# A hybrid sequence block on one core: the opening stage re-ordered, with its input rows turned on TensorE

## The chip, the core and the metric

The kernel runs on one core of a Trainium2 chip. The metric is the device time of one execution in microseconds (us), given as the median of three runs. The core's engines are TensorE (PE, matrix products), VectorE (DVE), ScalarE (ACT), GpSimd (POOL) and SyncE (SP, which here only issues transfers). Each engine works through its own list of instructions in order and waits where an operand or a buffer isn't ready.

## What is computed

One layer on x of 2048 rows by 1024: a norm of the rows, one combined projection, three groups (an mLSTM with gates, a pooling group, attention to 256 memory rows), an output projection and a final norm. What the change touches are the two norms and the memory's keys and values:

```
def rmsnorm(x, g):
    xf = x.astype(jnp.float32)
    y = xf * lax.rsqrt(jnp.mean(xf * xf, axis=-1, keepdims=True) + EPS)
    return (y * g.astype(jnp.float32)).astype(x.dtype)
...
    mn = rmsnorm(mem, mem_norm_g)
    kv = mn @ w_kv
    km, vm = jnp.split(kv, 2, axis=-1)
```

## The kernel before

**Products.** Each fp32 operand is split in two reduced-precision parts, hi (a copy, made by ACT) and lo (the difference to it, made by DVE), and each product is three matmuls: hi by hi, hi by lo, lo by hi (`mm3`, lines 150 to 156). A projection of a 1024x1024 block of x is cut into quarters A11, A12, A21, A22 (block of 512 rows by half of the 1024 columns), and done in seven products in place of eight: A11, A12, A22 and four sums of quarters, S1 to S4. With the blocks a, b (first) and c, d (second): S1 = c + d, which the code calls `e`; S2 = e - a; S3 = a - c; S4 = b - S2. The weights have forms of their own in the same way (T1 to T3, N4). Such a projection is a `Quad`; `TOK_ORDER` gives the order of its products, and a list `stream` sets when the forms of its weights are made (`pump`, `prep`).

**Halves.** The 2048 rows are done in two halves, s = 0 and s = 1. A half needs its seven forms of x, each [128 partitions, hi/lo, 512] in four pieces k; x stands there with columns on the partitions and rows along the free axis. The `y` tiles hold the unsplit quarters.

**Opening stage (lines 560 to 626).** It makes the forms of the first half and does one projection with them (`run_tok`), and the keys and values of the memory beside it. Memory comes transposed (`memT`, line 484), is split (490, 491) and squared (493), and the squares are summed by products with one column of ones (495). Rows of x come twice: once as rows for the sum of squares (`block_rows`, 500 to 507, ACT), once transposed (`load_y_raw`, line 178). `rsqrt_mean` (158 to 161) makes the factor of each row, with the power on POOL; `bcast` (163 to 169) puts the factors along the free axis by a product of diagonal tiles `dg` with ones, and `scale_y` (184 to 191) multiplies x by it on DVE. `x_split` (193 to 200) and `x_steps` (202 to 222) make the forms; POOL adds `e` and subtracts for S4, DVE does the other sums. Memory keys (`mem_k`, 525 to 530, four products of 24 matmuls) and values (`mem_v`, 541 to 548) lie between the products of x, hung on a count of products (`first(n)`, 596 to 622). The gates' product (`gates`, 450 to 476; one 16-column weight by A11, A12, S3 and A22) comes at the start of the next stage.

**What sets the order.** The program is written in this order, but a scheduler places the instructions of each engine, except those pinned by `keep_in_program_order`. PSUM tiles come from tags (`mm`, `pt`, `aux`), each with two buffers where the opening uses them. Working tiles are reused by tag, so a tile's next user waits for the last reader.

Of the kernel before, what the change touches and what calls it, by code (L numbers as in the profile page):

```python
# [18 lines left out]
P = 128  # L19
SEQ = 2048  # L20
# [32 lines left out]
def hybrid_block(tc, xT, xn, memT, wch, wuT, wtok, wgt, wkm, wvm, wo, pw, cols, bg, gf, out):  # L53
# [33 lines left out]
    with ExitStack() as outer:  # L87
# [18 lines left out]
        rm = const([P, MT], "rm")  # L106
        gat = const([P, NT, 8], "gat")
# [94 lines left out]
        def x_steps(y):  # L202
# [6 lines left out]
            return {  # L209
                "A11": lambda: x_split("A11", a),  # L210
# [13 lines left out]
        class Quad:  # L224
            def __init__(self, kind, s, i):
                self.kind, self.s, self.i = kind, s, i
                self.tok = kind == "tok"
                self.order = TOK_ORDER if self.tok else CH_ORDER
# [51 lines left out]
            def prep(self, f):  # L280
# [109 lines left out]
        def run_tok(q, step=None, pinned=False):  # L390
# [9 lines left out]
            for n, (xfm, wfm, acc, opens) in enumerate(q.order):  # L400
# [5 lines left out]
                for bk in range(2):  # L406
# [9 lines left out]
                    if n == 0:  # L416
                        s1[bk] = ev("s1")
                        A.activation(s1[bk], pf, AF.Copy)
                    elif n == 1:
# [3 lines left out]
                    elif n == 2:  # L423
                        u2[bk] = ev("u2")
                        V.tensor_tensor(u2[bk], pf, s1[bk], ALU.add)
                    elif n == 3:
                        V.tensor_tensor(s1[bk], pf, u2[bk], ALU.add)
                    elif n == 4:
# [5 lines left out]
                    elif n == 5:  # L434
# [15 lines left out]
        def gates(s):  # L450
            g1, g2 = bank([P, BW], "aux"), bank([P, BW], "aux")
            gs = [ev(f"gs{i}", tag="u2") for i in range(2)]

            def prod(pp, f, wt, k0, first, last):
                for k in range(4):
                    w = wt[:, (k0 + k) * 16:(k0 + k) * 16 + P]
                    T.matmul(pp, w, xf[f][k][:, 0], start=first and k == 0, stop=False, skip_group_check=True)
                    T.matmul(pp, w, xf[f][k][:, 1], start=False, stop=last and k == 3, skip_group_check=True)
            prod(g1, "A11", wgp, 0, True, True)
            ga = ev("ga")  # L460
            V.tensor_copy(ga[0:16], g1[0:16])
            prod(g2, "S3", wgn, 0, True, False)
            prod(g1, "A12", wgp, 4, False, True)
            V.tensor_copy(gs[0][0:16], g1[0:16])
            prod(g2, "A22", wgp, 4, False, True)
            V.tensor_tensor(gs[1][0:16], g2[0:16], ga[0:16], ALU.add)

            def finish_gates():
                for i in range(2):
                    b = 2 * s + i  # L470
                    pg = bank([P, 4, 8], "aux")
                    for t in range(4):
                        T.matmul(pg[:, t], gs[i][0:16, t * P:(t + 1) * P], e16[0:16], start=True, stop=True)
                    V.tensor_tensor(gat[:, 4 * b:4 * b + 4], pg, bgb.unsqueeze(1).to_broadcast([P, 4, 8]), ALU.add)
            return finish_gates
# [4 lines left out]
        def mem_load():  # L480
            pr = bank([P, MT], "pt")
            for i in range(4):
                raw = xslot(8 + i, [P, 2, NMEM], "mraw")
                dma(raw, memT[2 * i:2 * i + 2].rearrange("k p m -> p k m"))
# [111 lines left out]
        def first(n):  # L596
# [13 lines left out]
            elif 3 <= n < 7:  # L610
# [5 lines left out]
                if n < 5:  # L616
                    Wv.append(mem_w(wvm[n - 1], [P, 2, GW]))
# [647 lines left out]
```

## Time and profile before

| | us |
|---|---|
| median of three runs | 1221.77 (1220.72 to 1221.81) |
| profiled execution | 1220.8 |
| its span, first to last instruction | 1218.9 |
| PE busy | 1173.5 (96%) |
| DVE busy | 743.9 (61%) |
| ACT busy | 480.5 (39%) |
| POOL busy | 211.5 (17%) |
| mean granted clock of PE | 0.983 of full |

PE is the busy engine of the whole. The mean hides the stages: the profile's strip of 40 slices shows PE at six and seven tenths in the first three slices of 30 us and at nine in nearly all others, and the granted clock under full in those three alone. The views read below are windows of the span, the waits of PE by what ended them, and the timelines of the engines in the opening stage.

### The profile page before, as it was taken

How to read it: one execution, taken by the hardware profiler on the slowest of the kernel's cores; microseconds unless marked ns; L12 is line 12 of the kernel's file. 1: busy time of each engine (PE TensorE's matmuls, PEld its weight loads, DVE VectorE, ACT ScalarE, POOL GpSimd, SP SyncE). 2: the span in 40 equal slices, each digit the busy share in tenths (PEclk: the TensorE clock that was granted, in tenths of full speed). 3: DMA queues.
4: the chain of work that ended last, by engine and by line, in shares of the span. 5: the costliest groups of instructions: out<-in, count | busy, mean ns of one | idle time of the engine just before them, and what ended most of it. 6: DMA issues, size and time to landing. Idle time of an engine off the chain costs nothing. (4 is left out here: it accounts for less than half of the span.)

```text
span 1218.9 us, 17628 instructions
## 1 busy us (share of the span) xinstructions
PE 1173.5 (96%) x6579; PEld 1016.1 (83%) x6579; DVE 743.9 (61%) x1324; ACT 480.5 (39%) x947; POOL 211.5 (17%) x154
## 2 busy tenths in 40 slices
PE   6769999999999999999999999999999999999997
PEld 5759888887888998998788888888978888888886
DVE  5966587887777559633564554554546656556444
ACT  7534544444766444331311225555433223222211
POOL 1351121112001003100000000000054423233110
PEclk9879999999999999999999999999999999999999
DMA  9618788779555796546667776446695454554411
GB/s 350 233 44 299 265 293 281 259 276 324 211 195 182 256 390 226 181 140 228 198 219 241 240 244 226 154 155 223 214 325 188 137 184 154 172 165 151 144 52 69
DMA packets 124725, 258.75 MB, mean 212 GB/s; under 512 B 9824, under 2 KB 66400, under 8 KB 124384
## 3 DMA queue, kind: packets, MB, share of 16 engines
q1 hardware_dynamic: 83232, 226.17, 53.9%
q10 hardware_dynamic: 41408, 31.46, 8.1%
q8 instruction: 52, 0.85, 0.3%
q14 instruction: 33, 0.27, 0.1%
HBM read 158.96 MB, written 98.63 MB: 211 GB/s over the span
## 5 line engine op out<-in xcount | busy, mean ns | idle before, releaser
L307 ACT ACTIVATE wf<-wr 128x512 fp32r<-128x512 f32 x120 | 74.3, 627 | 106.7 <-PE mm L156 56.1
L308 DVE TENSOR_TENSOR wf<-wr,wf 128x512 fp32r<-128x512 f32 x120 | 84.8, 716 | 35.2 <-ACT wf L307 35.1
L152 PE MATMUL mm<-xS,wf 128*128 128x512 f32 x256 | 101.3, 396 | 1.9 <-DVE s L377 1.9
L156 PE MATMUL mm<-xS,wf 128*128 128x512 f32 x256 | 101.7, 397 | 0.0
L155 PE MATMUL mm<-xS,wf 128*128 128x512 f32 x256 | 101.0, 395 | 0.0
L1025 PE MATMUL mm<-woh,ybh 128*128 128x512 f32 x256 | 94.8, 405 | 0.0
L1025 PE MATMUL mm<-wol,ybh 128*128 128x512 f32 x256 | 92.8, 397 | 0.0
L1025 PE MATMUL mm<-woh,ybl 128*128 128x512 f32 x256 | 89.9, 394 | 0.0
L152 PE MATMUL mm<-xA,wf 128*128 128x512 f32 x224 | 88.6, 396 | 0.0
L156 PE MATMUL mm<-xA,wf 128*128 128x512 f32 x224 | 87.9, 393 | 0.0
L155 PE MATMUL mm<-xA,wf 128*128 128x512 f32 x224 | 87.7, 392 | 0.0
L1129 DVE SCALAR_TENSOR_TENSOR hh<-hh,ss,gz 128x128 f32<-128x128 f32 x64 | 52.4, 878 | 31.1 <-POOL ss L1127 31.1
L647 DVE SCALAR_TENSOR_TENSOR cacc<-text,col,cacc 128x1024 f32<-128x1024 f32 x48 | 65.5, 1374 | 6.7 <-ACT cacc L644 6.5
L996 POOL TENSOR_TENSOR ybl<-yr,ybh 128x1024 fp32r<-128x1024 f32 x16 | 39.2, 2450 | 173.2 <-ACT ybh L995 169.7
L291 POOL TENSOR_TENSOR wr<-wr 128x512 f32<-128x512 f32 (+1 forms) x16 | 27.2, 1697 | 198.8 <-DVE wf L308 180.4
L152 PE MATMUL pt<-wf,xS 128*128 128x256 f32 x192 | 55.7, 290 | 5.7 <-ACT xS L198 4.6
L156 PE MATMUL pt<-wf,xS 128*128 128x256 f32 x192 | 55.5, 289 | 5.2 <-DVE xS L199 5.2
L156 PE MATMUL mm<-wf,xA 128*128 128x256 f32 x192 | 56.3, 293 | 3.7 <-DVE xA L199 3.7
L152 PE MATMUL mm<-wf,xA 128*128 128x256 f32 x192 | 57.1, 297 | 2.0 <-DMA wf<-d_tok1B 2.0
L152 PEld LDWEIGHTS mm<-xS,wf 128*128 128x128 f32 x256 | 48.5, 189 | 12.0 <-DVE s L377 2.4
L156 PEld LDWEIGHTS mm<-xS,wf 128*128 128x128 f32 x256 | 48.6, 190 | 10.9
L155 PEld LDWEIGHTS mm<-xS,wf 128*128 128x128 f32 x256 | 48.5, 189 | 10.1
(314 smaller groups left out, 3251.3 us busy)
## 6 DMA issues: line engine op xcount, KB each, us to landing
wr<-in_wch_dram SPq DMA_DIRECT2D x20, 512.0 KB, 5.8
y<-in_xT_dram SPq DMA_DIRECT2D x32, 256.0 KB, 6.9
wr<-in_wtok_dram SPq DMA_DIRECT2D x16, 512.0 KB, 6.0
d_qk<-cacc ACTq DMA_DIRECT2D x32, 256.0 KB, 4.5
yr<-d_y SPq DMA_DIRECT2D x16, 512.0 KB, 4.7
qk<-d_qk SPq DMA_DIRECT2D x16, 512.0 KB, 4.1
gz<-d_t SPq DMA_DIRECT2D x16, 512.0 KB, 3.7
xr<-in_xn_dram SPq DMA_DIRECT2D x16, 512.0 KB, 3.6
```

What stands on the lines that cost most here:

```text
L152: ins = T.matmul(po, ah, bh, start=first, stop=False, skip_group_check=True)
L155: T.matmul(po, ah, bl, start=False, stop=False, skip_group_check=True)
L156: T.matmul(po, al, bh, start=False, stop=last, skip_group_check=True)
L291: G.tensor_tensor(B["B11"], B["B12"], B["B11"], ALU.subtract)
L307: A.activation(t[:, 0], part, AF.Copy)
L308: V.tensor_tensor(t[:, 1], part, r32(t[:, 0]), ALU.subtract)
L647: V.scalar_tensor_tensor(c, t[:, i:i + 2 * BW], w(i), c, ALU.mult, ALU.add)
L996: G.tensor_tensor(yl, yr, r32(yh), ALU.subtract)
L1025: T.matmul(outs[c][n], l, w[:, n * 512:(n + 1) * 512], start=i == 0 and p_ == 0, stop=i == KO - 1 and p_ == 2)
L1129: V.scalar_tensor_tensor(hh[:, h], hh[:, h], ss[:, h:h + 1], gz[:, 1, h], ALU.mult, ALU.mult)
```

## The change

- The first half's x is no longer loaded transposed. Its rows come once, 128 rows (512 KB) at a time. Their squares are summed alternately on ACT and on DVE, POOL makes the power, and DVE scales the rows where they are.
- PE turns the scaled rows, 128x128 at a time, into PSUM. From there ACT makes hi, DVE makes lo, and ACT makes a plain copy; the norm's weights are applied on the way. For the second block, DVE makes `e` straight from PSUM.
- The memory rows come, are scaled and are turned in the same way, after the second block of x.
- The first half's gate products of A11 and A12 follow the turning of the second block; those of S3 and A22 follow the opening's projection. In the second half both stand at the start of its stage.
- S1's product comes before S2's in the first projection.
- Memory keys and values come last; their weights are split in pieces of 512 instead of 1024.

Cut to its core:

```diff
+FIRST_ORDER = TOK_ORDER[:2] + (TOK_ORDER[3], TOK_ORDER[2]) + TOK_ORDER[4:]
...
-                self.order = TOK_ORDER if self.tok else CH_ORDER
+                self.order = CH_ORDER if not self.tok else TOK_ORDER if s or i else FIRST_ORDER
...
-                if f == "T2":
+                if f in ("T1", "T2") and "T1" not in B:
                     G.tensor_tensor(B["B11"], B["B12"], B["B11"], ALU.subtract)
                     B["T1"] = B["B11"]
+                if f == "T2":
...
+                    elif xfm in ("S2", "S1"):
+                        if xfm == "S2":
+                            u2[bk] = ev("u2")
+                            V.tensor_tensor(u2[bk], pf, s1[bk], ALU.add)
+                        if n == 3:
+                            V.tensor_tensor(s1[bk], banks["V"][bk].rearrange("p a b -> p (a b)"), u2[bk], ALU.add)
...
+        def gates_a(s):
+            g1 = bank([P, BW], "aux")
+            gate_prod(g1, "A11", wgp, 0, True, True)
+            ga[0] = ev("ga")
+            V.tensor_copy(ga[0][0:16], g1[0:16])
+            gate_prod(g1, "A12", wgp, 4, False, True)
+            gs = ev("gs", tag="u2") if s else xslot(19, [P, BW], "gs")
+            V.tensor_copy(gs[0:16], g1[0:16])
+            return gate_out(2 * s, gs)
+
+        def gates_b(s):
+            g2 = bank([P, BW], "aux")
+            gate_prod(g2, "S3", wgn, 0, True, False)
+            gate_prod(g2, "A22", wgp, 4, False, True)
+            gs = ev("gs", tag="u2")
+            V.tensor_tensor(gs[0:16], g2[0:16], ga[0][0:16], ALU.add)
+            return gate_out(2 * s + 1, gs)
...
+            def square(i):
+                junk = xslot(18 + (i % 2 if len(srcs) > 2 else 0), [P, D], "junk")
+                if i % 2:
+                    V.scalar_tensor_tensor(junk, rows[i], 1.0, rows[i], ALU.mult, ALU.mult, accum_out=sums[:, i:i + 1])
+                else:
+                    A.activation(junk, rows[i], AF.Square, accum_out=sums[:, i:i + 1])
+
+            def scale():
+                for j in range(0, len(srcs), 2):
+                    square(j)
+                    square(j + 1)
+                    rsqrt_mean(dst[:, j:j + 2], sums[:, j:j + 2], 2, D)
+                    for i in (j, j + 1):
+                        V.tensor_scalar(rows[i], rows[i], dst[:, i:i + 1], None, ALU.mult)
+            return rows, scale
...
+        def turn_rows(pt, rows, k):
+            for i, t in enumerate(rows):
+                ins = T.transpose(pt[:, i * P:(i + 1) * P], t[:, k * P:(k + 1) * P], ident)
+                if i == 0:
+                    tc.keep_in_program_order(ins)
...
+        def mem_load(rows):
+                pt = bank([P, 2, NMEM], "aux")
...
+                    turn_rows(pt[:, q], rows, k)
+                    A.activation(t[:, 0, q], pt[:, q], AF.Copy, scale=g)
+                    V.scalar_tensor_tensor(t[:, 1, q], pt[:, q], g, r32(t[:, 0, q]), ALU.mult, ALU.subtract)
...
+        def turned(rows, h):
+            for k in range(4):
+                pt = bank([P, BW], "pt" if k % 2 else "aux")
+                turn_rows(pt, rows, 4 * h + k)
+                yield k, pt, col[:, C_NG + 4 * h + k:C_NG + 4 * h + k + 1]
+
+        def block_form(y, rows, h):
+            f = ("A11", "A12")[h]
+            xf[f] = []
+            for k, pt, g in turned(rows, h):
+                t = xp.tile([P, 2, BW], F32R, name=f"x{f}_{k}", tag=f"x{4 * FORMS.index(f) + k}")
+                A.activation(t[:, 0], pt, AF.Copy, scale=g)
+                V.scalar_tensor_tensor(t[:, 1], pt, g, r32(t[:, 0]), ALU.mult, ALU.subtract)
+                A.activation(y[0][h][k], pt, AF.Copy, scale=g)
+                xf[f].append(t)
+
+        def block_y(y, rows, h, e=None):
+            for k, pt, g in turned(rows, h):
+                if e is not None:
+                    V.scalar_tensor_tensor(e[k], pt, g, y[1][0][k], ALU.mult, ALU.add)
+                A.activation(y[1][h][k], pt, AF.Copy, scale=g)
...
+        def mem_hl():
+            n = Wn[0]
+            Wn[0] += 1
+            hi = misc([P, 4 * P], "mwh", F32R, tag=f"ye{n % 2}")
+            lo = misc([P, 4 * P], "mwl", F32R, tag=f"ye{2 + n % 2}")
+            A.activation(hi, W[n], AF.Copy)
+            V.tensor_tensor(lo, W[n], r32(hi), ALU.subtract)
...
+        rows, scale = norm_rows([xn[t * P:(t + 1) * P] for t in range(4)], (4, 5, 6, 7), ssq[:, 0:4], rt[:, 0:4])
+        dma(col, cols)
         quads[0].load((0,))
+        rows1, scale1 = norm_rows([xn[t * P:(t + 1) * P] for t in range(4, 8)], (12, 13, 14, 15), ssq[:, 4:8], rt[:, 4:8])
+        dma(bgb, bg.partition_broadcast(P))
+        wgr = misc([P, KD, 8], "wgr")
+        dma(wgr, wgt)
+        load_upto(quads[0])
+        mrows, mscale = norm_rows([memn[i * P:(i + 1) * P] for i in range(MT)], (16, 17), ssm, rm)
+        for i in range(4):
+            mem_raw(wkm[i].rearrange("p a b -> p (a b)"), 20 + i)
...
+        scale()
+        pump(1)
+        block_form(y, rows, 0)
+        scale1()
+        block_form(y, rows, 1)
+        pump(2)
...
+            if n == 3:
+                block_y(y, rows1, 0)
+            elif n == 4:
+                block_y(y, rows1, 1, e)
+                xs["S1"]()
+                later(2, gates_a(0))
+                xs["S2"]()
+            elif n == 5:
+                mscale()
+                mem_load(mrows)
+            elif n == 6:
+                mem_k(0)
+            elif n == 7:
+                xs["S3"]()
+                mem_k(1)
+            elif n == 8:
+                mem_k(2)
+            elif n == 9:
+                mem_k(3)
+                for i in range(4):
+                    mem_raw(wvm[i].rearrange("p a b -> p (a b)"), 20 + i)
+            elif n == 10:
+                for q in range(4):
+                    mem_v(q)
+                xs["S4"]()
+            elif n == 11:
+                xs["A22"]()
...
         run_tok(next(it), pinned=True)
+        later(1, gates_b(0))
...
-            later(1, gates(s))
             if s:
+                later(1, gates_a(s))
+                later(1, gates_b(s))
```

The next listings show what stands in a row on an engine. In them `xA_0` is piece 0 of a quarter, `xS_0` of a sum, `wf` a split weight, `mhl` the split memory, `mwh` and `mwl` the split weights of memory.

PE at the start of the opening, before (the squares of memory, its first keys, the broadcast of the rows' factors, the first product of x):

```order
L495 MATMUL pt<-ones,msq 128x1 x16
L152 MATMUL mm<-mhl_143,mwh 128x256
L155 MATMUL mm<-mhl_143,mwh 128x256
L156 MATMUL mm<-mhl_143,mwl 128x256
...
L168 MATMUL aux<-dg,ones 128x512
...
L152 MATMUL mm<-wf,xA_0_281 128x256
L155 MATMUL mm<-wf,xA_0_281 128x256
L156 MATMUL mm<-wf,xA_0_281 128x256
```

PE at the start, after:

```order
L519 MATMUL aux<-ident,rows 128x128 x4
L519 MATMUL pt<-ident,rows 128x128 x4
L519 MATMUL aux<-ident,rows 128x128 x4
L519 MATMUL pt<-ident,rows 128x128 x4
L519 MATMUL aux<-ident,rows 128x128 x4
L519 MATMUL pt<-ident,rows 128x128 x4
L519 MATMUL aux<-ident,rows 128x128 x4
L519 MATMUL pt<-ident,rows 128x128 x4
L154 MATMUL mm<-wf,xA_0_212 128x256
L157 MATMUL mm<-wf,xA_0_212 128x256
L158 MATMUL mm<-wf,xA_0_212 128x256
```

Thirty-two transposes stand in the place of the memory's squares, keys and broadcast, and the product of A11 follows them directly.

DVE in the middle of the opening, where the sums of quarters are made, before (`ye` is `e`, `y_120` to `y_123` the pieces of a, `y_128` to `y_131` those of c):

```order
L191 SCALAR_TENSOR_TENSOR y_135<-y_135,col,aux 128x512
L308 TENSOR_TENSOR wf<-wr,wf 128x512 x2
L208 TENSOR_TENSOR y_128<-y_120,y_128 128x512
L199 TENSOR_TENSOR xS_0_775<-ye_136,xS_0_775 128x512
L208 TENSOR_TENSOR y_129<-y_121,y_129 128x512
L534 TENSOR_TENSOR kmt<-mm,rmb 128x256
L519 TENSOR_TENSOR mwl<-mwraw,mwh 128x1024
L208 TENSOR_TENSOR y_130<-y_122,y_130 128x512
L208 TENSOR_TENSOR y_120<-ye_136,y_120 128x512
L199 TENSOR_TENSOR xS_2_781<-ye_138,xS_2_781 128x512
```

DVE there, after:

```order
L554 SCALAR_TENSOR_TENSOR ye_138<-aux,col,y_130 128x512
L210 TENSOR_TENSOR y_128<-y_120,y_128 128x512
L554 SCALAR_TENSOR_TENSOR ye_139<-pt,col,y_131 128x512
L210 TENSOR_TENSOR y_129<-y_121,y_129 128x512
L201 TENSOR_TENSOR xS_0_494<-ye_136,xS_0_494 128x512
L210 TENSOR_TENSOR y_130<-y_122,y_130 128x512
L201 TENSOR_TENSOR xS_1_497<-ye_137,xS_1_497 128x512
L210 TENSOR_TENSOR y_120<-ye_136,y_120 128x512
L477 COPY ga<-aux 16x512
L210 TENSOR_TENSOR y_131<-y_123,y_131 128x512
L201 TENSOR_TENSOR xS_2_500<-ye_138,xS_2_500 128x512
L210 TENSOR_TENSOR y_121<-ye_137,y_121 128x512
```

The four sums of `e` are now DVE's, and the copy `ga`, for which PE's gate products wait, stands among the sums and splits.

PE between the last memory keys and the product of S2, before:

```order
L152 MATMUL mm<-mhl_188,mwh 128x256
...
L152 MATMUL aux<-mwh,mhl_143 128x512
...
L152 MATMUL pt<-wf,xS_0_668 128x256
L155 MATMUL pt<-wf,xS_0_668 128x256
L156 MATMUL pt<-wf,xS_0_668 128x256
```

PE there, after (the gates of A12, S1's first bank, the turning of the memory, S2's first bank, S1's second):

```order
L460 MATMUL aux<-xA_3_293,wgp 128x512
L463 MATMUL aux<-xA_3_293,wgp 128x512
L154 MATMUL mm<-wf,xS_0_494 128x256
L157 MATMUL mm<-wf,xS_0_494 128x256
L158 MATMUL mm<-wf,xS_0_494 128x256
...
L154 MATMUL mm<-wf,xS_3_503 128x256
L157 MATMUL mm<-wf,xS_3_503 128x256
L158 MATMUL mm<-wf,xS_3_503 128x256
L519 MATMUL aux<-ident,rows 128x128 x14
L469 MATMUL aux<-e_78,gs 128x8 x4
L154 MATMUL pt<-wf,xS_0_535 128x256
L157 MATMUL pt<-wf,xS_0_535 128x256
L158 MATMUL pt<-wf,xS_0_535 128x256
```

S1 has its second bank behind the turning of memory; keys and values of memory follow later.

## Rows read from the trace of the kernel before

**Rows 1.** Table of windows: length; busy (instructions) by engine; granted clock; DMA share; GB/s

```profile
8.00:12.00 4.00, 2.94 (x13) 2.68 (x13) 3.01 (x6) 4.00 (x9) 0.00 (x0) 1.00 1.03 417
0.00:40.00 40.00, 27.02 (x140) 25.13 (x141) 23.86 (x51) 27.67 (x54) 7.20 (x12) 0.91 0.95 356
40.00:80.00 40.00, 24.97 (x135) 21.72 (x134) 36.44 (x52) 16.62 (x27) 23.06 (x9) 0.74 0.40 121
80.00:120.00 40.00, 40.00 (x289) 37.71 (x288) 24.72 (x40) 16.39 (x28) 5.54 (x5) 1.00 0.60 211
```

**Rows 2.** Waits of PE, 0 to 140 us: total us, times, longest

```profile
PE pt L495 <- ACT msq L493: 8.2, 6, 6.3
PE pt L156 <- DVE xS L199: 5.2, 3, 4.2
PE aux L168 <- DVE dg L166: 5.2, 1, 5.2
...
PE mm L156 <- DVE xA L199: 3.7, 2, 3.4
```

**Rows 3.** The same view, 140 us to the end, one row of the longest

```profile
PE mm L152 <- DMA wf<-d_tok1B: 2.0, 1, 2.0
```

**Rows 4.** Timeline of PE: start, duration, line, operation, count

```profile
16.48 0.41 PE L155 MATMUL mm<-mhl,mwh 128*128 128x256 f32 x1
...
30.58 0.42 PE L152 MATMUL mm<-wf,xA 128*128 128x256 f32 x1
...
34.84 0.36 PE L156 MATMUL mm<-wf,xA 128*128 128x256 f32 x1
...
87.14 0.28 PE L152 MATMUL mm<-wf,xS 128*128 128x256 f32 x1
...
89.97 0.39 PE L152 MATMUL aux<-mwh,mhl 128*128 128x512 f32 x1
...
92.69 0.28 PE L152 MATMUL mm<-wf,xS 128*128 128x256 f32 x1
...
114.27 0.39 PE L457 MATMUL aux<-xA,wgp 128*128 128x512 f32 x1
...
955.29 0.60 PE L1134 MATMUL aux<-ident,hh 128*128 128x128 f32 x4
955.72 1.06 PE L1083 MATMUL aux<-qk 128*128 128x128 f32 x8
```

**Rows 5.** Timeline of ACT, first 10 us

```profile
4.09 1.28 ACT L490 ACT_TABLE_LOAD   x1 [4.09 <-DMA mraw<-in_memT_dram]
...
6.81 1.69 ACT L490 ACTIVATE mhl<-mraw,col 128x256 fp32r<-128x256 f32 x4
```

**Rows 6.** Timeline of DVE, opening stage and two later places

```profile
7.34 1.68 DVE L491 SCALAR_TENSOR_TENSOR mhl<-mraw,col,mhl 128x256 fp32r<-128x256 f32 x4 [0.22 <-ACT mhl L490]
...
40.45 1.21 DVE L294 TENSOR_TENSOR wt<-wr 128x1024 f32<-128x1024 f32 x1
...
43.06 3.09 DVE L519 TENSOR_TENSOR mwl<-mwraw,mwh 128x1024 fp32r<-128x1024 f32 x1
...
52.17 5.36 DVE L191 SCALAR_TENSOR_TENSOR y<-y,col,aux 128x512 f32<-128x512 f32 x8 [0.16 <-PE aux L168]
...
60.37 1.77 DVE L208 TENSOR_TENSOR y<-y,y 128x512 f32<-128x512 f32 x1
...
72.22 1.28 DVE L199 TENSOR_TENSOR xS<-y,xS 128x512 fp32r<-128x512 f32 x2
...
592.52 2.47 DVE L647 SCALAR_TENSOR_TENSOR cacc<-text,col,cacc 128x1024 f32<-128x1024 f32 x2
...
1214.74 0.88 DVE L1172 TENSOR_SCALAR xo<-qk,fs 128x512 f32<-128x512 f32 x2 [0.74 <-POOL fs L1168]
```

**Rows 7.** Timeline of POOL, opening stage

```profile
41.81 3.26 POOL L300 TENSOR_TENSOR wr<-wr,wt 128x1024 f32<-128x1024 f32 x1 [1.90 <-DVE wt L294]
...
66.16 14.61 POOL L208 TENSOR_TENSOR y<-y,y 128x512 f32<-128x512 f32 x4 [4.57 <-DVE y L208]
```

More of the change, by code (lines that the diff above doesn't have):

```diff
@@ L209, in x_steps @@
             return {
+                "e": e,
                 "A11": lambda: x_split("A11", a),
@@ L448, in run_tok @@
                     tick()
[L450 to L475, printed above, removed]
@@ L478, in hybrid_block, with gate_prod @@
-        mhl = []
-        def mem_load():
-            pr = bank([P, MT], "pt")
+        ga = [None]
+        def gate_prod(pp, f, wt, k0, first, last):
+            for k in range(4):
+                w = wt[:, (k0 + k) * 16:(k0 + k) * 16 + P]
+                ins = T.matmul(pp, w, xf[f][k][:, 0], start=first and k == 0, stop=False, skip_group_check=True)
+                if k == 0:
+                    tc.keep_in_program_order(ins)
+                T.matmul(pp, w, xf[f][k][:, 1], start=False, stop=last and k == 3, skip_group_check=True)
@@ new lines, in gate_out, with run @@
+        def gate_out(b, gs):
+            def run():
+                pg = bank([P, 4, 8], "aux")
+                for t in range(4):
+                    T.matmul(pg[:, t], gs[0:16, t * P:(t + 1) * P], e16[0:16], start=True, stop=True)
+                V.tensor_tensor(gat[:, 4 * b:4 * b + 4], pg, bgb.unsqueeze(1).to_broadcast([P, 4, 8]), ALU.add)
+            return run
+        def gates_a(s):
[7 more added lines that the diff above has]
+            return gate_out(2 * s, gs)
@@ new lines, in gates_b, with norm_rows @@
+        def gates_b(s):
[5 more added lines that the diff above has]
+            return gate_out(2 * s + 1, gs)
+        mhl = []
+        def norm_rows(srcs, slots, sums, dst):
+            rows = []
+            for i, src in enumerate(srcs):
+                t = xslot(slots[i], [P, D], "rows")
+                dma(t, src)
+                rows.append(t)
+            def square(i):
[12 more added lines that the diff above has]
+            return rows, scale
@@ L489, in mem_load @@
                     g = col[:, C_MG + k:C_MG + k + 1]
-                    A.activation(t[:, 0, q], raw[:, q], AF.Copy, scale=g)
-                    V.scalar_tensor_tensor(t[:, 1, q], raw[:, q], g, r32(t[:, 0, q]), ALU.mult, ALU.subtract)
-                    sq = xslot(6 + q, [P, NMEM], "msq")
-                    A.activation(sq, raw[:, q], AF.Square)
-                    for m in range(MT):
-                        ins = T.matmul(pr[:, m:m + 1], sq[:, m * P:(m + 1) * P], ones[:, 0:1],
-                                       start=k == 0 and m == 0, stop=k == KD - 1, skip_group_check=True)
-                        tc.keep_in_program_order(ins)
@@ new lines, in block_y, with mem_raw @@
+        def block_y(y, rows, h, e=None):
[3 more added lines that the diff above has]
+                A.activation(y[1][h][k], pt, AF.Copy, scale=g)
+        W, Wn = [], [0]
+        def mem_raw(src, tag):
+            raw = xslot(tag, [P, 2, 4 * P], "mwraw")
+            dma(raw.rearrange("p a b -> p (a b)"), src)
+            for i in range(2):
+                W.append(raw[:, i])
@@ L531, in mem_k_out @@
[L531 to L537 removed]
+            for half in range(2):
+                hi, lo = mem_hl()
+                for kk in range(4):
+                    k = 4 * half + kk
+                    t = mhl[k // 2]
+                    sl = slice(kk * P, kk * P + P)
+                    mm3(pp, hi[:, sl], lo[:, sl], t[:, 0, k % 2], t[:, 1, k % 2], k == 0, k == KD - 1, pin=kk == 0)
```

130 lines of the change are left out of this document (26 added, 104 removed).

## The prediction

> **What bounds the kernel now.** I read the table of windows first, for what is left to gain. In the first 40 us TensorE (PE) is busy 27.0 us, in the next 40 only 25.0, from 80 to 120 all 40.0 [rows 1]. So 28 us of idle PE time lie in the opening stage, and the granted clock of its second window, 0.74, says that part of the busy time ran at 1.2 GHz. I then read the waits of PE in the first 140 us: 8.2 us on the squares of the memory tokens, 5.2 on DVE's `dg`, 5.2 and 3.7 on the lo splits of x [rows 2]. PE waits for DVE and ACT, which turn x into split, normalised forms. Behind 140 us its longest single waits are 2.0 [rows 3]. Last comes the first gate product at 114.27 [rows 4]: the opening's last product, A22, ends there. As PE hardly rests after it, the opening's end moves the span one for one, if the work on either side of it is counted.
>
> **The mark to compare with.** The changed program puts 40 matmuls of 512 columns before the end of A22 that stood behind it: 16 of the gates and 24 of the next projection. Twelve such take 2.72 us (89.97 to 92.69), 0.227 each [rows 4], so 40 are 9.1. Equal time would thus be an A22 that ends at 114.3 + 9.1 = 123.4.
>
> **First leg, to the end of A12.** Removed: 32 one-column products of squares, three broadcasts of `rt`/`rm` over `dg`, 16 loads of x transposed and 16 scalings of them. Added: 80 transposes of 128x128; four took 0.43 (955.29 to 955.72), 0.11 each, 8.6 us in all [rows 4]. Rows of x land first; in before the first load lets ACT go at 4.09 [rows 5] and 417 GB/s flow at 8 to 12 us [rows 1], so a 512 KB row block comes each 1.26 us: 4.2, 5.5, 6.9, 8.2. Squares, power and scaling of two blocks and the next squares keep DVE until 10.7. From there DVE has no gap: 6 scalings of 1024, 3 squares of 1024, 8 lo splits from PSUM, 6 weight splits, two weight sums of 1024 and crumbs.
> Prices: a tensor by a scalar, 512 wide, 0.44 (two in 0.88), so 0.72 for 1024, which no row shows; its ends are 0.67 (what a fixed part in the 0.44 would leave) and the two-operand 1.13. I take the low one's side, as the 512 row is the same form. A square with its sum, STT 1024: 1.2 (two in 2.47). A lo split, STT 512 out of PSUM: 0.66 (eight in 5.36). A weight split 0.60 (two plain two-operand ones in 1.28, the tail counted once), a weight sum 1.13 (40.45 on, 1.21 to its end) [rows 6].
> Sum: 4.3 + 3.6 + 5.3 + 3.6 + 2.3 + 0.6 = 19.7, so A12's last lo stands at 30.4.
> PE turns 32 tiles meanwhile, in four banks of PSUM that come free only when hi, lo and plain copy have been read one behind the other, and is done at 22.4. A11's 48 products of 256 columns would take 5.7 at full clock (24 in 2.83, from 87.14 to 89.97). After gaps I expect 1.2 GHz: in before, after a wait, the pitch is 0.213 (20 steps from 30.58 to 34.84), and 0.118 later [rows 4]. About 5 us of that cost 2.2: A11 runs from 22.6 to 30.5. A12's first bank ends at 33.3, then 16 transposes (1.8), then the second bank (2.8): 37.9.
>
> That the transposes don't raise the clock is taken from the nearest row: behind ten microseconds of one-column products the memory keys started at 0.213 too (16.48 on) [rows 4]. The Trainium skill, "TensorE: Matmul & The Clock Gate", Part 4 (PE-mode transpose), says more: a transpose does not count as busy for the clock in the way a matmul does. By that, turning x on PE puts cold time before A11, which speaks against the change. If instead the 32 transposes warm PE, the sum falls by the 2.2 us above. No row here decides it.
>
> **Second leg, to the second bank of S1.** The 16 gate products of A11 and A12 stand directly behind the turning of the second block. Their copy `ga` stands on DVE behind the four e sums, four of the plain differences and two splits, and the gate's second half waits for it: PE is idle from 41.5 to 45.7. The DVE list of the e sums, S1 and S2 has 26 instructions of 0.60 to 0.66 [rows 6] and runs from 38.2 to 54.1; S1's first bank fits in, to 52.8. Then memory: each of four banks holds two 256-wide tiles; hi is read by ACT (0.40, four in 1.69) [rows 5], lo by DVE (0.40, four in 1.68) [rows 6], one behind the other: 1.6 a bank, 6.4 in all, and what stands between, so S1's second bank starts at 60.6. Much of the old wait for DVE is back here in another place.
>
> **Third leg, PE-bound.** S1's second bank, S3, S4, 16 products with `pwr` and A22 took from 92.69 to 114.27 in before, 21.6 [rows 4]; S2's rest 4.4; memory keys, 96 products of 256, 11.3; memory values, 48 of 512, 10.9; the 24 of the next stage 5.5: 53.7. To it come 2.2 for a second cold start, and 1.8 where memory values wait for their weights: each 512-wide half is split (0.60 on ACT, then 0.60 on DVE) in two alternating buffers, 1.2 against 1.36 of PE per half, so any other DVE work in between shows. End: 60.6 + 57.7 = 118.3.
>
> **What the trace leaves open: POOL against DVE.** While POOL works on full tensors, DVE can stall: a 1.21 us split took 3.09 (43.06) under POOL's 41.81, and a 0.60 sum 1.77 (60.37). But under POOL's four sums from 66.16 to 80.8, DVE kept its pace (two in 1.28 at 72.22) while POOL took 3.65 each [rows 6, 7]. The change keeps two 1024-wide POOL operations and four 512-wide ones on the DVE path. Bounds: nothing, and 2 x 1.9 + 4 x 1.15 = 8.4. I take 1.4, nearer nothing, since the four sums go with the pattern of 66.16 and PE hides a part of leg one's. End 119.7 against 123.4: a gain of 3.7.
>
> **The second half.** Its gates, which stood as fillers between products, now stand together at the start of its stage. The work is equal; a filler that is gone can open a wait of up to 2 us, as PE's longest waits there show [rows 3], and a better order may save as much. I take zero, with 2 either way. Memory keys and values land later but are read only after the next projection: nothing.
>
> **The sum.** The profiled execution took 1220.8 (span 1218.9 and 1.9 around it), so 1217.1 against it; the median of the three runs is 1221.8, which gives 1218.1. I state 1217.5.
>
> **Rivals.**
> - *POOL holds DVE (slower).* If each of the six POOL operations falls on the DVE chain at full price, 118.3 + 8.4 = 126.7: 3.3 worse than 123.4, so 1224 to 1225. It decides from 5.1 us on. For it: before lost 1.9 and 1.1 us in two such rows of the same stage [rows 6]. Against it: PE covers some of the places. Scaling at 1.13 (8 on the chain, 0.41 each) would add 3.3 and reach the same side.
> - *Nothing within what can be told.* The gain is real but POOL takes 2 more, or the second half gives 2 back: 1220 to 1222. For it: PE's waits reappear at `ga` and the memory bank turning, 4.2 and 6.4 us.
> - *A larger gain.* Transposes warm the clock (2.2), the two memory banks overlap (3), the values' weights never show (1.8), POOL costs nothing (1.4): 8.4 more, 1209; half of it, 1213. For it: DVE kept its pace at 66.16. Against it: all four have to fall well.
> - *The change doesn't do what it says:* if the opening were still bound by arrival, the loads' order would decide. But eight row blocks, four weight blocks and two of memory are 7.3 MB, 18 us at 417 GB/s [rows 1], and DVE needs the last of them only near 30. I give this no time of its own.
>
> **Chances and range.** The forecast, 1214 to 1219.4: 0.40; the larger gain, 1208 to 1214: 0.15; nothing, 1219.4 to 1224.2: 0.25; slower, above that: 0.20. A measurement of this kernel tells 0.2%, 2.4 us, from no change. That gives faster 0.55, same 0.25, slower 0.20. Leaving out a tenth on each side, the range goes from 1209 (everything in the larger gain) to 1226.
>
> **What would show it.** The first product line should start near 22.5 at half clock; the gates of A12 end about 48; the memory transposes stand between 54 and 60; A22 end near 119.7; windows from 80 us on stay at 40.0. Wrong would be: DVE rows of scaling well over 0.75; DVE splits of over 2 us under POOL; a start of A11 before 19 or at full clock; a wait of PE behind 125 us that before does not have.

## The result and the profile after

The change made the kernel slower. The median of four executions is 1242.89 us (1241.4 to 1244.18) against 1221.24 of before on the same chip: ratio 1.0179 [1.0162, 1.0197], or 21.7 us more, well outside the range of 1209 to 1226. The profiled execution took 1243.63 us. The page of the kernel after, span and TensorE (PE):

```profile
span 1241.8 us, 17701 instructions
...
PE 1190.1 (96%) x6621; PEld 1021.1 (82%) x6621; DVE 747.4 (60%) x1326; ACT 486.0 (39%) x956; POOL 201.7 (16%) x152
```

PE was busy 1173.5 us of 1218.9 before, so the span grew by 22.9 and PE's busy time by 16.6. The 80 added transposes kept PE busy for 16.8 us (46 of them ran at the lower clock, four in 1.06), and the 38 products that they replace for 11.6, which leaves 11.4 of the 16.6. So much of the loss is not waiting: PE works longer on the same products. The tables of windows show where. Kernel after (length; busy of PE, weight load, DVE, ACT, POOL with instructions; granted clock; DMA share; GB/s):

```profile
0.00:40.00 40.00, 23.31 (x145) 21.02 (x146) 31.51 (x53) 26.85 (x46) 11.28 (x15) 1.00 0.72 271
40.00:80.00 40.00, 27.73 (x155) 24.54 (x154) 28.98 (x45) 17.96 (x34) 11.47 (x4) 0.74 0.11 36
80.00:120.00 40.00, 40.00 (x271) 36.49 (x270) 27.45 (x44) 18.60 (x33) 3.09 (x3) 1.00 0.59 196
460.00:500.00 40.00, 32.53 (x259) 30.76 (x259) 40.00 (x58) 17.89 (x32) 11.94 (x8) 1.00 0.67 238
520.00:540.00 20.00, 20.00 (x171) 20.00 (x170) 9.97 (x14) 8.20 (x14) 4.76 (x2) 1.00 0.32 109
```

Kernel before, the last two of these:

```profile
460.00:500.00 40.00, 37.38 (x286) 35.62 (x285) 37.35 (x57) 17.62 (x30) 12.16 (x9) 0.96 0.65 224
520.00:540.00 20.00, 20.00 (x179) 20.00 (x178) 7.51 (x12) 8.00 (x14) 0.00 (x0) 1.00 0.44 143
```

The first three answer to [rows 1]. They show an opening with as much idle PE as before (16.7 and 12.3 us, against 13.0 and 15.0). The fourth shows a hole that the prediction did not have: at the start of the second half PE idles 7.5 us, in before 2.6. The fifth is the odd one. PE is busy all 20 us in both kernels, at granted clock 1.00 in both, and yet does 171 products instead of 179. The timeline of PE there (start, duration, line, operation), before:

```profile
159.82 0.39 PE L156 MATMUL mm<-xS,wf 128*128 128x512 f32 x1
...
165.32 0.39 PE L155 MATMUL pt<-xA,wf 128*128 128x512 f32 x1
...
519.77 0.28 PE L155 MATMUL pt<-wf,xA 128*128 128x256 f32 x1
...
531.10 0.28 PE L152 MATMUL mm<-wf,xA 128*128 128x256 f32 x1
```

After:

```profile
159.81 0.39 PE L158 MATMUL pt<-xS,wf 128*128 128x512 f32 x1
...
165.41 0.39 PE L158 MATMUL mm<-xA,wf 128*128 128x512 f32 x1
...
519.79 0.28 PE L158 MATMUL pt<-wf,xS 128*128 128x256 f32 x1
...
531.63 0.28 PE L154 MATMUL pt<-wf,xA 128*128 128x256 f32 x1
```

Between the first two rows lie 24 products of 512 columns without a gap, between the last two 100 of 256. The pitch is 229.2 ns before and 233.3 after for the wide ones, 113.3 and 118.4 for the narrow ones. The durations are equal; only the distance from start to start tells. From 130 us on the kernel has about 1950 wide and 1640 narrow back-to-back products of these tiles, and 380 of the output's; 3.4 to 4.4 ns on each wide one and 2.9 to 3.5 on each narrow one (mean pitches) make 7.1 + 5.1 + 1.5 = 13.7 us. So the question to the experiments was what makes the same matmul slower, and what the other 8 us are.

### The profile page after: what moved, and what is told of

It is laid out like the page before. It is cut to its first block, busy times and chain, and to the rows that moved or that the text cites. A ratio compares the mean times of both kernels' runs of the same rounds, so it can differ in the third digit from the quotient of the medians.

```text
span 1241.8 us, 17701 instructions
## 1 busy us (share of the span) xinstructions
PE 1190.1 (96%) x6621; PEld 1021.1 (82%) x6621; DVE 747.4 (60%) x1326; ACT 486.0 (39%) x956; POOL 201.7 (16%) x152
## 4 chain that ended last, share of the span: by engine, by line
PE 84%; DVE 8%; DMA 4%; ACT 2%; issue 1%; SPq 0%; POOL 0%; ACTq 0%; POOLq 0%; DVEq 0%
PE mm L1071 20%; PE mm L154 11%; PE mm L158 11%; PE mm L157 11%; PE pt L154 6%; PE pt L157 5%; PE pt L158 5%; PE aux L157 1%; PE aux L158 1%; PE aux L154 1%; PE aux L1129 1%; PE pt L1144 1%; PE pt L1143 1%; DMA y<-in_xT_dram 1%; PE aux L1149 1%
## 5 line engine op out<-in xcount | busy, mean ns | idle before, releaser
L154 PE MATMUL mm<-wf,xS 128*128 128x256 f32 x192 | 56.1, 292 | 2.3 <-issue 2.3
L154 PE MATMUL mm<-wf,xA 128*128 128x256 f32 x192 | 55.1, 287 | 3.0 <-DMA wf<-d_tok1B 3.0
L154 PE MATMUL pt<-wf,xS 128*128 128x256 f32 x192 | 55.6, 290 | 1.5 <-DVE u L430 1.0
L158 PE MATMUL mm<-wf,xA 128*128 128x256 f32 x192 | 54.6, 285 | 2.4 <-DVE xA L547 2.4
```

The source lines that it names most:

```text
L154: ins = T.matmul(po, ah, bh, start=first, stop=False, skip_group_check=True)
L158: T.matmul(po, al, bh, start=False, stop=last, skip_group_check=True)
```

## Experiments

Times are medians, with the ratio to before on the same chip. Three causes are told apart: the **place of the tiles**, the **gates of the second half**, and the **opening**.

### The place of the tiles

The change declares one small constant more, `ssm` of two columns, between `rm` and `gat`. In the built program it takes a slot of 32 bytes in each partition, and every tile behind it moves by 32: the first weight tile `wf` from byte 7072 to 7104. The split forms of x are allocated from the other end and stay (byte 96 modulo 128). The first pair of runs moves the tiles back in after, and moves them in before.

e1_after_tiles_back, the kernel after with both constants in one slot:

```diff
-        rm = const([P, MT], "rm")
-        ssm = const([P, MT], "ssm")
+        rmss = const([P, 2 * MT], "rm")
+        rm, ssm = rmss[:, 0:MT], rmss[:, MT:2 * MT]
```

> The changed kernel with the new constant `ssm` put into the unused half of `rm`'s 32-byte slot, so that every tile behind it (the weights `wf` first) stands at the address it has in the kernel before (7072 instead of 7104 bytes into the partition for the first `wf`); order of work unchanged. Theory of place: products with `wf` of 512 columns go back from a pitch of 233.3 ns to 228.9, those of 256 from 118.3 to 113.3 in the second half, and the time falls by 12 to 15 us, to 1228 to 1231. Rival, the pitch hangs on the order of instructions or on the traffic beside them: pitch and time stay, 1243.

Measured: 1229.12, ratio 1.0083 [1.0054, 1.0111]. The timeline of PE in e1, again with 100 products from the first row to the second:

```profile
519.73 0.28 PE L154 MATMUL mm<-wf,xS 128*128 128x256 f32 x1
...
531.07 0.28 PE L157 MATMUL mm<-wf,xA 128*128 128x256 f32 x1
```

The pitch is 113.4 again. By the ratios, 0.96% of 1221 came back, 11.7 us (within some 4), with no instruction added or removed.

e2_before_shift32, the kernel before with nothing but an unused tile:

```diff
         rm = const([P, MT], "rm")
+        const([P, MT], "pad")
         gat = const([P, NT, 8], "gat")
```

> The kernel before with one more constant of 2 columns, never used, between `rm` and `gat`: all tiles behind it move by 32 bytes, as in the changed kernel; nothing else. Theory of place: pitch 233.3 and 118.3 as in the changed kernel, time up by 12 to 15 us, 1233 to 1236. Rival, order or traffic: 1221, pitch 228.9 and 113.3.

Measured: 1231.78, 1.0093 [1.0062, 1.0123], pitches 233.3 and 118.3. An unused tile of 32 bytes costs before 11.4 us. So the place of the tiles is shown from both sides, at a little less than the 12 to 15 us that the pitches promised.

e3_before_shift64 (the same with `const([P, 16], "pad")`) and e8_before_shift96 (`const([P, 24], "pad")`) ask for the period; e4_before_x_shift32 moves the x forms and not the weights, by a pool that opens ahead of theirs at their end of the memory:

```diff
+        qcm, qp = pool("qp", side="right")
+        qp.tile([P, 8], F32, name="pad", tag="pad")
         xcm, xp = pool("xp", side="right")
```

> The same with an unused constant of 16 columns, a move by 64 bytes. If what counts is the address modulo 64: 1221 and pitch 228.9. If any move of the tiles does it (a fit of larger blocks, or more than 64 bytes): 1233 to 1236.

> The kernel before with the x forms (allocated from the other end) moved down by 32 bytes, `wf` left where it is, so that the two operands of a product differ by 32 modulo 64. If the difference of the two operands counts: pitch 233 and 1233 to 1236. If the place of `wf` alone counts: 1221. If a place at 32 modulo 64 is good for each operand by itself: slower too, and only a run with both moved tells it from the first.

> The kernel before with an unused constant of 24 columns: all tiles behind it move by 96 bytes, so that `wf` and x differ by 32 modulo 128 (0 in e3, 64 in before, 96 in e2, e4 and the changed kernel). If a difference that is no multiple of 64 is dear in either direction: 233.3 and 118.3, 1231. If only 96 is dear: 1219 to 1221.

e11_before_both_32 has the edits of e2 and e4 together, which move the two operands by 32 bytes in opposite directions:

> The kernel before with both moves of e2 and e4 at once: `wf` 32 bytes up, the x forms 32 bytes down, so that both stand at 64 modulo 128 and their difference is 0, as in e3, while neither stands where it did in before or e3. Theory, the difference of the two operands counts: pitch 226.7 for 512 columns and 120.0 for 256 as in e3, time 1218 to 1221. Rival, each operand has to stand at 32 modulo 64: both are off, 233 and 118.3 or worse, 1231 or more.

Measured, with the kernels above; the third column, the distance, is (address of `wf` minus address of x) modulo 128, the pitches are from the same stretches of the timeline, and the ratios of after and e1 hold the other two causes too:

| kernel | moved | wf − x | 512 wide, ns | 256 wide, ns | ratio to before |
|---|---|---|---|---|---|
| before, e1 | – | 64 | 229, 229 | 113.3, 113.4 | 1, 1.0083 |
| after | wf +32 | 96 | 233.3 | 118.4 | 1.0179 |
| e2 | wf +32 | 96 | 233.3 | 118.3 | 1.0093 [1.0062, 1.0123] |
| e4 | x −32 | 96 | 233.3 | 118.3 | 1.0087 [1.0060, 1.0114] |
| e8 | wf +96 | 32 | 233.3 | 117.8 | 1.0074 [1.0057, 1.0090] |
| e3 | wf +64 | 0 | 226.8 | 120.0 | 0.9982 [0.9966, 0.9998] |
| e11 | wf +32, x −32 | 0 | 226.7 | 119.9 | 0.9971 [0.9956, 0.9986] |

e3, two of its rows of 256 columns, 100 products apart:

```profile
519.83 0.28 PE L157 MATMUL mm<-wf,xS 128*128 128x256 f32 x1
...
531.83 0.28 PE L153 MATMUL mm<-wf,xA 128*128 128x256 f32 x1
```

e4 gives the pitch of e2 though it moves other tiles, and e11, which adds two moves that each cost 11 us, costs nothing. So it is the distance of the two operands that counts and not the place of either. e3 refuted a period of 64 bytes: at distance 0 the wide products are the fastest of all and the narrow ones the slowest, and the two nearly cancel. Four distances were run, 32 bytes apart; no run moved a tile by 128, so that the period is 128 is not shown.

Nor does the distance alone set the pitch. At distance 64 the narrow products have two paces. The kernel before itself, in the same view as above, does 172 of them in 20 us at granted clock 1.00 in an earlier stretch (pitch 117.8), against 179 later (113.3):

```profile
420.00:440.00 20.00, 20.00 (x172) 20.00 (x171) 9.66 (x15) 5.80 (x11) 4.80 (x2) 1.00 0.99 351
```

The profile of e7 below, whose tiles stand where those of e1 do, has 172 from 520 to 540 too. At distance 96 (after, e2, e4) the narrow products have the slow pace in both places.

### The gates of the second half

The new helper `gate_prod` pins the first of each pair of gate products to its place in the program. In before the scheduler was free to put the second half's gates into waits of PE. e5_free_gates is e1 with the pin in the first half only (the four calls pass `not s`):

```diff
-        def gate_prod(pp, f, wt, k0, first, last):
+        def gate_prod(pp, f, wt, k0, first, last, pin=True):
...
-                if k == 0:
+                if k == 0 and pin:
                     tc.keep_in_program_order(ins)
```

> e1 (the changed kernel with its tiles at the addresses of before), and in the second half the gate products are no longer pinned, so that the scheduler puts those of A11, A12 and S3 back between the products that wait near 460 to 500 us. Theory, the gates were a filler for waits there: PE's idle time between 465 and 505 us falls from 6.7 to about 2.6 us, and 32 products of 0.23 (7.3 us) leave the start of the next stage: about 5 us less than e1, 1224. Rival, the order is indifferent because the waits end later by as much: 1229.

Measured: 1223.62, 1.0032 [1.0015, 1.0049]; 0.51% or 6.2 us better than e1. PE's idle time from 460 to 500 us is 4.0 us in e5 (before 2.6, after 7.5). e12_before_gates_pinned is the counter-test, before with the pin in the second half:

```diff
-                    T.matmul(pp, w, xf[f][k][:, 0], start=first and k == 0, stop=False, skip_group_check=True)
+                    ins = T.matmul(pp, w, xf[f][k][:, 0], start=first and k == 0, stop=False, skip_group_check=True)
+                    if s and k == 0:
+                        tc.keep_in_program_order(ins)
```

> The kernel before with the second half's gate products pinned to the start of their stage, as the changed kernel has them; the opening stage and all places untouched. Theory, they were a filler for waits near 460 to 500 us: PE's idle time between 460 and 500 us goes from 2.6 to 6 or 7 us, and the time up by 4 to 6 us, 1225 to 1227. Rival, what e5 won came from other shifts of the changed kernel: 1221.

Measured: 1227.64, 1.0046 [1.0022, 1.0071], 5.6 us. The waits of PE from 440 to 500 us in e12 (total us, times, longest):

```profile
PE mm L152 <- DMA wf<-d_tok1B: 3.5, 2, 1.9
PE mm L152 <- issue: 2.5, 1, 2.5
PE pt L152 <- DVE s L430: 1.2, 1, 1.2
```

The same stretch of before has one wait of 2.0 on that DMA [rows 3] and one of 0.6. The waits of after, 440 to 640 us, are those of e12:

```profile
PE mm L154 <- DMA wf<-d_tok1B: 3.0, 2, 1.8
PE mm L154 <- issue: 2.3, 1, 2.3
PE pt L154 <- DVE s L435: 1.2, 2, 0.8
```

In before the gates were run among these products (the first at 460.1, those of S3 from 488.0). The pin takes the filling out and adds nothing: PE's idle time from 460 to 500 us is 7.3 in e12 against 2.6, which is most of the 5.6.

### The opening

What is left, ratio 1.0032 or 3.9 us, is put down to the opening by subtraction. In after the first gate product of S3, which follows A22's end, stands at 126.77, where the prediction's mark for equal time is 123.4: 3.4 late. In e1 and e5, which have the same opening, it stands at 127.45 and 126.48, so single profiles differ by about 1 us here.

e6_s1_first is e5 with the scaling and turning of the memory (`mscale`, `mem_load`) one step later, so that S1's second bank follows its first:

```diff
-            elif n == 5:
+            elif n == 6:
                 mscale()
                 mem_load(mrows)
-            elif n == 6:
                 mem_k(0)
```

> e5 with the turning of the memory rows hung one step later, so that the second bank of S1 stands ahead of it on PE, in place of behind it. Theory, the second leg of the prediction is where the opening loses: S1's second bank (2.8 to 5 us of work at either clock) runs in the 5.2 us in which PE waits for DVE at the second memory bank, and 3 us are won: 1221. Rival, DVE's list sets the end of the memory turning, and PE waits there as long as it did, for the keys: within 1 us of e5.

Measured: 1218.83, 0.9988 [0.9970, 1.0007]. S1 now runs without a gap, yet the turning of the memory still waits for DVE; timeline of PE in e6:

```profile
62.44 1.11 PE L519 MATMUL aux<-ident,rows 128*128 128x128 f32 x4 [4.70 <-DVE mhl L533]
```

S3's first gate product came 1.15 us earlier than in e5 (125.33 against 126.48), the profiled execution took 2.3 less, and the ratios differ by 0.44%, 5.4 us, with intervals of about 2 us each. That it is better is shown; how much of it lies in the opening is not, as the 1.15 is hardly more than what profiles of one opening differ by.

e7_no_pool_sums is e5 without POOL's four differences for S4 (S4 is split from `b_` as it stands, so that part of the product is left out). The line stands in `x_steps`, which both halves use, so the second half loses its four as well (in e5 they run from 479 to 489 us):

```diff
-                "S4": lambda: (each(G, b_, b_, a, ALU.subtract), x_split("S4", b_)),
+                "S4": lambda: x_split("S4", b_),
```

> e5 without the four differences that POOL makes for S4 (left out: S4 is split from b itself, so the output is not the reference's). Theory, POOL's four operations from 47.8 to 59.2 us hold DVE, whose rows of 0.67 took 1.74 there three times: the rows go back to 0.67, the memory turning starts about 3.2 us earlier and the time is 1221. Rival, other work on DVE or ACT takes the place: 1224, with the rows of DVE back at 0.67 all the same.

Measured: 1217.68, 0.9975 [0.9962, 0.9988], by the ratios 7.0 us better than e5. That holds both halves and can't be put down to the opening. There, DVE's first lo of the memory stands 9.0 us behind its copy `ga`, in e5 12.8, and S3's first gate product at 124.17, 2.3 earlier than in e5. DVE in e7 (timeline):

```profile
55.55 0.67 DVE L571 TENSOR_TENSOR mwl<-mwraw,mwh 128x512 fp32r<-128x512 f32 x1
56.15 0.67 DVE L201 TENSOR_TENSOR xS<-y,xS 128x512 fp32r<-128x512 f32 x1
56.76 0.67 DVE L571 TENSOR_TENSOR mwl<-mwraw,mwh 128x512 fp32r<-128x512 f32 x1
```

These are the rows that take 1.74 to 1.76 in after (below). POOL's sums held them. The expectation of e9, below, takes the whole gain of e7 for that of the opening.

e9_s4_late is e6 with the first half's S4 differences computed into other tiles (tag `y10`, which the second block's first half and then the split memory values use), so that POOL cannot start them before those come free:

```diff
+            def s4():
+                out = [misc([P, BW], "y4", tag=f"{s4tag}{k}") for k in range(4)] if s4tag else b_
+                for k in range(4):
+                    G.tensor_tensor(out[k], b_[k], a[k], ALU.subtract)
+                x_split("S4", out)
...
-                "S4": lambda: (each(G, b_, b_, a, ALU.subtract), x_split("S4", b_)),
+                "S4": s4,
```

> e6 with POOL's four differences for S4 written to the buffers of the second block's first half, which come free only after S3's split, so that POOL starts them behind the turning of the memory rows; nothing left out. Theory from e7 (1217.7 against 1223.6 in e5 with these four left out): the hold-up of DVE's rows before the memory turning goes and 2 to 4 us are won over e6: 1215 to 1217. Rival, POOL holds DVE just as long at the later place, where the splits of the memory's weights wait, or S4's split comes late for its product: 1219 or more.

Measured: 1218.29, 0.9969 [0.9953, 0.9985]. POOL in e9, and DVE beside it (timeline):

```profile
110.76 5.94 POOL L210 TENSOR_TENSOR y<-y,y 128x512 f32<-128x512 f32 x4 [14.05 <-DMA d_vm<-vmhl]
...
114.01 1.54 DVE L201 TENSOR_TENSOR xS<-y,xS 128x512 fp32r<-128x512 f32 x1 [0.15 <-ACT xS L200]
115.70 1.55 DVE L201 TENSOR_TENSOR xS<-y,xS 128x512 fp32r<-128x512 f32 x1 [0.15 <-ACT xS L200]
```

The four take 5.94, in after 11.47, and it is DVE that is held: rows of 0.68 take up to 1.55. But PE has A22's product to run there and doesn't wait, and the second bank of the memory turning starts 2.8 us earlier than in e6 (59.62 against 62.44). This kernel computes everything, and it is faster than after and than before: 3.8 us less than before. Against e6 the ratios differ by 0.19%, 2.3 us, which is less than their intervals together, so the forecast 2 to 4 us is not shown. That 3.8 is near the gain of the prediction (3.7) is chance: e9 has changes of order that the predicted kernel hasn't. e10_s4_late_64 adds `const([P, 16], "pad")` to bring it to distance 0:

> e9 with an unused constant of 16 columns, a move of `wf` by 64 bytes as in e3, so that the two operands of a product stand at the same place modulo 128. Theory of place: 512-column products fall from a pitch of 228.9 to 226.7, those of 256 in the second half rise from 113.3 to 120.0, together 1 to 2 us less than e9 as e3 stood to before: 1213.5 to 1216. Rival: the two sorts balance, equal to e9.

Measured: 1218.35, 0.9975 [0.9962, 0.9989]: no difference from e9.

## Why the prediction was wrong, step by step

**The account.** By the ratios, the loss of 1.79% is 0.96 of place (after to e1), 0.51 of second-half gates (e1 to e5) and 0.32 of opening (e5 to before): 11.7 + 6.2 + 3.9 us, the first two within some 4, the third within 2. The counter-tests in before give 11.4 (e2) and 5.6 (e12), and the traces give 3.1 to 4.1 for the opening.

**The step that failed first is one that isn't there.** The prediction adds up instructions removed, added and moved; the declaration of `ssm` issues nothing and was not among them, hence costed at nothing. It cost 11.4 to 11.7 us, more than either of the other two causes. No row of before shows a price for it; it could only have been bounded by asking whether the operands of the matmuls keep their addresses. The premise "the opening's end moves the span one for one" fell with it: the rest of the program was not the same work at the same speed. The sign that the prediction gave, "windows from 80 us on stay at 40.0", held from 80 to 120 and hid the loss, since a slower PE is just as busy. Two of its signs of being wrong did come: "a wait of PE behind 125 us that before does not have" (the waits of after from 440 to 640 us above) and "DVE rows of scaling well over 0.75" (3.56 for two at 26.40, below).

**The second half, "zero, with 2 either way".** The mechanism was named (a filler that is gone opens a wait) and mis-sized: 5.6 to 6.2. It was bounded by the longest single wait in [rows 3], which is what was left with the fillers in place. The price of losing a filler is what it now covers, and several waits can open, not one.

**First leg.** The timeline of PE in after:

```profile
22.62 0.56 PE L154 MATMUL mm<-wf,xA 128*128 128x256 f32 x1
...
25.75 0.35 PE L158 MATMUL mm<-wf,xA 128*128 128x256 f32 x1
...
48.24 0.79 PE L460 MATMUL aux<-xA,wgp 128*128 128x512 f32 x1 [3.91 <-DVE ga L477]
...
60.82 1.12 PE L519 MATMUL aux<-ident,rows 128*128 128x128 f32 x4 [5.16 <-DVE mhl L533]
63.02 1.11 PE L519 MATMUL aux<-ident,rows 128*128 128x128 f32 x4 [1.09 <-DVE mhl L533]
...
71.59 0.56 PE L154 MATMUL mm<-wf,xS 128*128 128x256 f32 x1
...
126.77 0.40 PE L460 MATMUL aux<-xS,wgn 128*128 128x512 f32 x1
```

A11 starts at 22.62, predicted 22.6. From its second product (22.98) to 25.75 the pitch is 0.213, that of the lower clock; at 0.118 the 14 steps to 25.75 would have been 1.5 shorter, where I took 2.2. (The column of the granted clock says 1.00 for these 3 us, but the trace's record of the clock begins only at 25.9; from 60.8 to 73, at the same pitch, it says 0.50.) So in this execution the 32 transposes ahead of A11 did not raise the clock. In others they did. PE in e7, where nothing but the same transposes has run before these rows:

```profile
18.10 0.66 PE L519 MATMUL aux<-ident,rows 128*128 128x128 f32 x4 [1.54 <-ACT y L548]
...
22.18 0.37 PE L154 MATMUL mm<-wf,xA 128*128 128x256 f32 x1
22.39 0.28 PE L157 MATMUL mm<-wf,xA 128*128 128x256 f32 x1
```

Four transposes took 0.66 there, in after 1.11, and A11 ran at the higher clock from its start. The last transposes ahead of A11 ran so in e5 and e10 too (24.09 and 22.44), and those of e1 from 18.34, though its clock had fallen again when A11 began. The Trainium skill, "TensorE: Matmul & The Clock Gate", Part 4 (PE-mode transpose), by which a transpose doesn't count as busy for the clock in the way a matmul does, agrees with after and not with e1, e5, e7 and e10, and the measurement decides. The warm start, which the prediction had in its larger gain, thus comes in some executions and not in others.

Scaling a 1024 row at 0.72 was right: 0.71 in the rows where POOL rests (two in 1.42 at 8.00, 12.13, 19.00 and 36.10). But A12's last lo ended at 33.6, not 30.4, for which POOL stands beside DVE. DVE in after:

```profile
19.00 1.42 DVE L514 TENSOR_SCALAR rows<-rows,rt 128x1024 f32<-128x1024 f32 x2
...
20.99 1.67 DVE L162 TENSOR_SCALAR ms<-ssq 128x2 f32<-128x2 f32 x1
...
26.40 3.56 DVE L514 TENSOR_SCALAR rows<-rows,rt 128x1024 f32<-128x1024 f32 x2
...
54.67 1.76 DVE L571 TENSOR_TENSOR mwl<-mwraw,mwh 128x512 fp32r<-128x512 f32 x1
56.36 1.74 DVE L201 TENSOR_TENSOR xS<-y,xS 128x512 fp32r<-128x512 f32 x1
58.03 1.74 DVE L571 TENSOR_TENSOR mwl<-mwraw,mwh 128x512 fp32r<-128x512 f32 x1
...
60.30 0.47 DVE L533 SCALAR_TENSOR_TENSOR mhl<-aux,col,mhl 128x256 fp32r<-128x256 f32 x1
```

POOL in after, with the four sums of 47.75 once as one row and once as a group (shortest, median and longest in ns):

```profile
20.07 2.56 POOL L294 TENSOR_TENSOR wr<-wr 128x1024 f32<-128x1024 f32 x1 [2.01 <-ACT y L548]
...
25.47 3.27 POOL L304 TENSOR_TENSOR wr<-wr,wt 128x1024 f32<-128x1024 f32 x1 [2.04 <-ACT junk L506]
...
47.75 11.47 POOL L210 TENSOR_TENSOR y<-y,y 128x512 f32<-128x512 f32 x4 [11.69 <-DVE y L210]
L210 POOL TENSOR_TENSOR y<-y,y x4: 1704/1720/6449, 47.8 to 57.5; 128x512 f32<-128x512 f32 x4
```

The group of [rows 7] in before, from 66.16:

```profile
L208 POOL TENSOR_TENSOR y<-y,y x4: 1273/1282/10895, 66.2 to 79.5; 128x512 f32<-128x512 f32 x4
```

**The POOL term, 1.4 with bounds of 0 and 8.4.** DVE lost 2.1 on the scalings at 26.40, 1.5 on a 2-column crumb at 20.99 (elsewhere 0.17), 3.2 on three rows from 54.67: 6.8, near the upper bound. I took the value near nothing because of the pattern of [rows 7], where POOL was the one to wait, "3.65 each". That was a misreading: 3.65 is the mean of one sum of 10.89, beside which DVE kept its pace, and of three of 1.28, which ran when DVE's list had ended (75.91). So the rows had no price for the other three beside a busy DVE. In after the first sum takes 6.45 while DVE keeps 0.60 a row (48 to 53), and the other three, 1.70 to 1.73 each, hold DVE's rows from 54.67. The bound was right and the choice wrong. The Trainium skill, SBUF — State Buffer, "SBUF: two separate sides", says that the port the two engines share is held for a whole instruction and the other then blocks; the rows agree that one of them stalls, though POOL's first sum waited through some nine DVE rows and not one. e7 shows that POOL's sums hold the three rows; the scalings and the crumb, which POOL's 25.47 and 20.07 stand beside, no run takes apart, and none shows what decides which engine waits.

**Second and third leg.** The wait at `ga` was foreseen (3.9; predicted 4.2). DVE's list began at 40.7 (38.2) and ended at 60.3 (54.1): 2.5 from the first leg, the rest POOL's. A memory bank turned in 2.2, not 1.6, with the turning and the reads of ACT and DVE one behind the other and PE at granted clock 0.50 from 60.8 to 73. S1's second bank began at 71.6, not 60.6; S2's first bank had been put ahead of it, so the third leg was shorter, 55.2 against 57.7. So of the 11.0 by which S1's second bank is late, 2.5 come from the first leg, 3.7 from POOL, 2.5 from S2's bank and the rest, about 2, from the memory banks and the small gate products behind them. With the shorter third leg, 11.0 − 2.5 − 1.4 (the POOL term that the forecast already held) = 7.1, the difference between 119.7 and 126.77. The waits of PE in after, 0 to 140 us, answer to [rows 2]:

```profile
PE aux L519 <- DVE rows L514: 12.2, 4, 8.8
PE aux L519 <- DVE mhl L533: 7.3, 3, 5.2
PE aux L460 <- DVE ga L477: 3.9, 1, 3.9
```

**The rivals.** "POOL holds DVE", 1224 to 1225, describes the opening as it came out (3.4 to 3.9 late), and e5, which has only that, took 1223.62 (3.9 more than before by its ratio). The result went past it for two reasons that no rival named.

**What stays open.** Why the distance of two operands sets the pace, and whether its period is 128; what else does, as in before itself the same tiles ran in some stretches at 117.8 and 231 (the mean of its narrow products from 130 us on is 115.1, not 113.3); why e10 gains nothing over e9 where e3 stands 0.2% below before; and where the part of e6's gain lies that S3's first gate product does not show. The profiles of before and after have three stretches of about 3.4 us at granted clock 0.50 between 130 and 1210 us (before at 281, 465 and 844, after at 285, 500 and 866), those of e5, e6 and e10 none; what they are worth in the ratios was not taken apart.

## What to carry to other kernels

Before the cost of an edit is summed, compare the addresses of the large operands in the two built programs: a new constant of a few bytes in front of everything moves them all, and a constant put into an existing slot moves none. Read the pitch of back-to-back matmuls, not their durations or PE's busy share, in a stretch that the change doesn't touch; if it differs, the edit has a cost that no list of instructions holds. An instruction that is pinned may have been a filler: its price is the waits that it used to cover, and the waits that remain beside it are no bound for that.

## What the runs showed of the hardware

Back-to-back fp32 products with a stationary and a moving operand in SBUF ran at a pitch that changes with the distance of the two operands' addresses. In the stretches compared it was, at 512 columns, 227 ns at distance 0, 229 at 64 and 233.3 at 32 and 96 (the distance counted modulo 128 bytes, four values run); at 256 columns 120 at 0, 113.3 or 117.8 at 64, and about 118 at 32 and 96, all at granted clock 1.00. In this kernel that is 11 us of 1221 for a move of 32 bytes. Transposes of 128x128 alone brought TensorE from the lower to the higher clock in e1, e5, e7 and e10, and did not in after. A DVE instruction of two columns took 1.67 us in place of 0.17 beside a POOL operation. Of POOL's four equal sums of 128x512 the first took 6.45 us (10.89 in before) while DVE ran its rows back to back, and the next three 1.7 each while DVE's rows went from 0.67 to 1.75.
